# Nine instead of six feature tiles of an up projection by seven products, with sums and differences made sooner

## The chip, the cores and the metric

One NeuronCore of a Trainium2 chip runs the whole kernel in one launch. The metric is the device time of one execution in microseconds; the time before is the median of three runs.

## The reference

A hybrid encoder block on x of 512 positions by 1024 features in float32: three token mixers, merged and projected, then a gated feed-forward network with a convolution over the positions, then a norm. The change lies in the feed-forward part and the output projection ahead of it:

```python
x = x + merged @ w_out[l]
x = x + conv_glu_ffn(rms_norm(x, ffn_norm_g[l]), w_ffn_up[l], w_ffn_conv[l], b_ffn_conv[l], w_ffn_down[l])
return rms_norm(x, final_norm_g)

def conv_glu_ffn(h, w_up, w_conv, b_conv, w_down):
    a, u = jnp.split(h @ w_up, 2, axis=-1)        # 1024 -> 2 x 2816
    return (jax.nn.gelu(dwconv3(a, w_conv, b_conv)) * u) @ w_down
```

## The kernel before

**Arithmetic.** Every float32 product is made by three fp32r matmuls: each operand is split into a high part (a copy rounded by ACT) and a low part (the difference, by DVE), and `mm3` (L370 to L372) adds high x high, high x low and low x high. A weight block comes by an SP load into a raw buffer `wr` (three of them), is split into a `w` buffer (four of them) by ACT (L336) and DVE (L337), and is read by PE.

**Up projection.** The 2816 features of the gate half a (`ua`) and of the other half u (`uu`) are cut into 22 feature tiles f of 128. An ordinary tile takes 24 matmuls of 128x512 for `ua` and 24 for `uu`. Then comes the tail of the tile: the convolution (`conv`, L570 to L574), gelu on ACT (L1451), a multiplication with the norm's factor `rb2` on POOL, the product with u on DVE (L1467 or L1469), and from f = 12 on a split into UH and UL (L376, L377). Since a is done before u, most of the tail runs beside the `uu` matmuls.

A tile in `SUP` goes another way (`up_seven`): a and u are together a matrix product of 2 x 2 blocks (two halves of the features summed over, two halves of the positions, a and u), which seven products of half size replace, 7 x 12 = 84 matmuls of 128x256. Four of its weight operands are sums of blocks: `up_load` brings the first summand by SP into a tile `ut`, `up_sum` adds the second by an accumulating DMA on POOL's queue, and a fifth is a difference made on DVE. The differences of x are made once, by `x_forms(p)` for p = 0 to 3 (two ACT copies; DVE L1341, L1342, L1343; an ACT copy; DVE L1346, L1347), into units `xf`. In a tile of this kind a and u are complete only at its end.

**Down projection.** 62 blocks of `w_ffn_down` in the order `DOWN`: a "k" block multiplies one tile of UH/UL, an "s" block is part of a seven-product scheme over the first 12 tiles, some with an accumulated weight. Loads go out up to nine blocks ahead, into `wr` and then into quarters of *units* (14 buffers of 2112 floats a partition, `unit()`), which are also the home of x, its splits, its differences and the results. The first four blocks have six matmuls each. The residual is turned on the chip and kept in DRAM (`turn_out`, 64 KB stores) and brought back by eight 256 KB loads (`turn_in`, "U<-td" in the profile) for the sum at the end.

**What sets the order.** Each engine and each DMA queue issues in the order printed below; a scheduler places instructions by their place in the program and by what they wait for. `in_turn` keeps one engine's operations in program order. SP issues nearly all loads: a load that waits for its buffer holds back what stands behind it.

Of the kernel before, what the change touches and what calls it, by code (L numbers as in the profile page):

```python
# [25 lines left out]
NSP = 6  # L26
NOK = FT - 2 * NSP
HELD = 4
SUP = (5, 7, 9, 11, 13, 15)
UP_ORDER = (1, 2, 4, 5, 7, 3, 6)  # L30
HC = D // 2
NU = 14
# [105 lines left out]
def hybrid_block(ctx, tc, xT, memT, wflat, vecs, gbias, nabias, out):  # L138
# [21 lines left out]
    def scr(n=512):  # L160
        return sp.tile([P, 512], F32, tag="scr", name=nm("s"))[:, :n]
# [36 lines left out]
    def rstd_row_turned(u, tag):  # L198

        v, col, row = tiny(NT), tiny(32), tiny(32)  # L200
        G.memset(col, 0.0)
        V.tensor_reduce(v, u, axis=AX.XY, op=ALU.add)
        V.tensor_scalar(v, v, 1.0 / D, EPS, op0=ALU.mult, op1=ALU.add)
        G.tensor_tensor(col[:, :NT], v, nhalf[:, :NT], op=ALU.pow)
# [5 lines left out]
        SY.dma_start(rb, d.partition_broadcast(P))  # L210
        return rb

    def by4(a):
# [46 lines left out]
        q = slice(j * HC, (j + 1) * HC)  # L260
        return lw[0][:, q], lw[1][:, q]

    ur, uf = [], {}

    chain = {}

    def in_turn(eng, what, *a, **k):

        with tc.issue_after(chain[eng]) if eng in chain else ExitStack():
            chain[eng] = getattr({"V": V, "A": A, "G": G}[eng], what)(*a, **k).ins  # L270

    def emit_sum(i):

# [1038 lines left out]
    for f in range(KT):  # L1312
        xr = scr()
        SY.dma_start(xr, xT[:, f, :])
        ps = proj(("out", f), GH, GL)
        V.tensor_tensor(x2[f], ps, xr, op=ALU.add)
        split_act(HH[f], HL[f], x2[f], vcol("ffn_g", f))
        if f == 0:
            A.activation(acc2, x2[f], AF.Square)
        else:  # L1320
            sq = scr()
            A.activation(sq, x2[f], AF.Square)
            G.tensor_tensor(acc2, acc2, sq, op=ALU.add)


    x2v = [u[:, :4 * S].rearrange("p (f s) -> p f s", f=4) for u in x2u]
    ur.extend(unit() for _ in range(NSP // 2))
    ou, UH, UL = [], [], []
    res, turns = {}, {}
    xf = [unit(F32R) for _ in range(5)]  # L1330
    XF = (5, 2, 6, 7, 1)
    uw = {}

    def x_forms(p):

        y, d = ur[2][:, p % 2 * D:(p % 2 + 1) * D], ur[1][:, :5 * M]
# [4 lines left out]
        V.tensor_tensor(d5[:, 0:2], y4[:, 0:2], y4[:, 2:4], op=ALU.subtract)  # L1341
        V.tensor_tensor(d5[:, 2:4], y4[:, 1:3], y4[:, 0:4:3], op=ALU.subtract)  # L1342
        V.tensor_tensor(d5[:, 4], y4[:, 0], y4[:, 3], op=ALU.subtract)  # L1343
        h = xf[p][:, :5 * M]
        A.activation(h, d, AF.Copy)
        V.tensor_tensor(xf[p][:, 5 * M:8 * M], d[:, :3 * M], h[:, :3 * M].bitcast(F32), op=ALU.subtract)  # L1346
        V.tensor_tensor(xf[4][:, p * S:(p + 1) * S], d[:, 3 * M:], h[:, 3 * M:].bitcast(F32), op=ALU.subtract)  # L1347

    def x_of(i, p):

        if FORMS[i][1] is None:
            th, k = FORMS[i][0]
            q = slice(th * M, (th + 1) * M)
            return HH[2 * p + k][:, q], HL[2 * p + k][:, q]
        j = XF.index(i)
        lo = xf[p][:, (5 + j) * M:(6 + j) * M] if j < 3 else xf[4][:, p * S + (j - 3) * M:p * S + (j - 2) * M]
        return xf[p][:, j * M:(j + 1) * M], lo

    def up_load(f):

        for i in UP_ORDER:
            if ("ut", f, i) in BINDEX:
                off = BINDEX["ut", f, i][1]
                src = wflat[off:off + P * 2 * HC].rearrange("(p n) -> p n", p=P)
                r = tp.tile([P, S], F32, tag="E", name=nm("ut"), bufs=EB)
                SY.dma_start(r, src[:, :HC])
                uw[f, i] = r, src[:, HC:]

    def up_sum(f):
# [7 lines left out]
    def up_weight(f, n):  # L1377
# [13 lines left out]
        V.tensor_tensor(l, src, h.bitcast(F32), op=ALU.subtract)  # L1391
        uw[f, "w", i] = h, l

    def up_seven(f):

        b12, b45, b7, b36 = [atps() for _ in range(4)]
        at = {1: b12[:, :M], 2: b12[:, M:], 4: b45[:, :M], 5: b45[:, M:], 7: b7[:, :M], 3: b36[:, :M], 6: b36[:, M:]}
        ta, tu = scr(), scr()
        t00, t01, t11 = ta[:, :M], tu[:, :M], tu[:, M:]
        for n, i in enumerate(UP_ORDER):  # L1400
            if n + 2 < len(UP_ORDER):
                up_weight(f, n + 2)
            elif n + 2 == len(UP_ORDER):
                emit_split(st["split"])
                st["split"] += 1
            wh, wl = uw.pop((f, "w", i))
            for p in range(KT // 2):
                c = slice(p * P, (p + 1) * P)
                xh, xl = x_of(i, p)
                mm3(at[i], wh[:, c], wl[:, c], xh, xl, p == 0, p == KT // 2 - 1)  # L1410
            if i == 2:
                A.activation(ta, b12, AF.Copy)
                A.activation(t11, at[2], AF.Copy, scale=-1.0)
                V.tensor_tensor(t11, t11, at[1], op=ALU.add)
            elif i == 5:
                A.activation(t01, at[5], AF.Copy, scale=-1.0)
                t2 = ta.rearrange("p (u s) -> p u s", u=2)
                V.tensor_tensor(t2, t2, at[4].unsqueeze(1).to_broadcast([P, 2, M]), op=ALU.add)
                V.tensor_tensor(t00, t00, at[5], op=ALU.add)
            elif i == 7:  # L1420
                V.tensor_tensor(t00, t00, at[7], op=ALU.add)
            elif i == 6:
                V.tensor_tensor(tu, tu, b36, op=ALU.add)
                V.tensor_tensor(t11, t11, at[3], op=ALU.add)
        uw.pop(f)
        return ta, tu
    for f in range(FT):
        if f == 0:
            wa, wu = weights(("ua", f)), weights(("uu", f))
            pa, pu = mmps(), mmps()  # L1430
            for k in range(KT - 1):
                mm3(pa, wa[k][0], wa[k][1], HH[k], HL[k], k == 0, False)
            for k in range(KT - 1):
                mm3(pu, wu[k][0], wu[k][1], HH[k], HL[k], k == 0, False)
            t2 = turn_in(turn_out(by4(acc2)), "nab", 2)
            k = KT - 1
            mm3(pa, wa[k][0], wa[k][1], HH[k], HL[k], False, True)
            mm3(pu, wu[k][0], wu[k][1], HH[k], HL[k], False, True)
            pa1 = proj(("ua", 1), HH, HL, bank=atps)
            rb2 = rstd_row_turned(t2, "2")  # L1440
            pu1 = proj(("uu", 1), HH, HL, bank=atps)
        elif f in SUP:
            pa, pu = up_seven(f)
        else:
            if f + 1 in SUP:
                up_sum(f + 1)
            pa = pa1 if f == 1 else proj(("ua", f), HH, HL)
        if f + 2 in SUP:
            up_load(f + 2)
        c = conv(pa, rb2, "ffw", "ffb", f, FT)  # L1450
        A.activation(c, c, AF.Gelu_apprx_tanh)  # L1451
        if "G" not in chain:
            chain["G"] = G.tensor_tensor(c, c, rb2, op=ALU.mult).ins
        else:
            in_turn("G", "tensor_tensor", c, c, rb2, op=ALU.mult)
        if f < KT // 2:
            x_forms(f)
        if f > 0 and f not in SUP:
            if f + 1 in SUP:
                ws = weights(("uu", f))  # L1460
                uw[f + 1] = split.pop(BINDEX["ub", f + 1][0])
                for n in range(2):
                    up_weight(f + 1, n)
                split[BINDEX["uu", f][0]] = ws
            pu = pu1 if f == 1 else proj(("uu", f), HH, HL)
        if f < 2 * NSP:
            V.tensor_tensor(ur[f // 4][:, f % 4 * S:(f % 4 + 1) * S], pu, c, op=ALU.mult)  # L1467
        else:
            V.tensor_tensor(c, pu, c, op=ALU.mult)  # L1469
# [277 lines left out]
```

## Time and profile before

| | |
|---|---|
| median of three runs | 851.2 us (850.47 to 851.59) |
| profiled execution | 851.33 us, span 849.6 us, granted clock 0.999 |
| PE busy | 841.0 us (99% of the span) |
| DVE, ACT, POOL busy | 622.4, 476.4, 175.6 us |
| DMA | 147.32 MB, mean 173 GB/s |
| output projection | about 451.2 to 494.7 us |
| up projection | about 494.7 to 731.22 us |
| down projection | from 731.22 us |

How to read it: a row of a windows table is the window in us from the span's start, its length, then busy time and count of PE, PEld, DVE, ACT and POOL, the granted clock as a share, the share in which the DMA engines were busy, and GB/s. A row of a timeline is start, duration, engine, line, operation, output<-inputs; in brackets the engine's idle time ahead and what ended it. The rows of the chain of waits have start, duration, engine and operation. The rows of DMA issues have count, KB each and the median time from issue to landing.

### The profile page before, as it was taken

To read this page: it belongs to the slowest core of one execution; us is meant where nothing else is said; L and a number is where in the kernel's file an instruction comes from. 1 tells how busy PE (TensorE), PEld (TensorE's weight loads), DVE (VectorE), ACT (ScalarE), POOL (GpSimd) and SP (SyncE) were. 2 spreads that over 40 slices of the span, in tenths; PEclk is the share of its full clock that TensorE was granted. 3 is DMA by queue.
4 is the path that set the end of the run, shared out by engine and by line. 5 is a ranking of instruction groups with operands and counts; after the bars stand their busy time and mean duration, and the time that the engine had idled before them with its cause. 6 is when DMAs were issued, how large, how long until landed. Compare 5 with 4: busy or idle time off the path is not lost.

```text
span 849.6 us, 12743 instructions
## 1 busy us (share of the span) xinstructions
PE 841.0 (99%) x4214; PEld 716.3 (84%) x4214; DVE 622.4 (73%) x1246; ACT 476.4 (56%) x992; POOL 175.6 (21%) x268
## 2 busy tenths in 40 slices
PE   9999999999999999999999999999999999999997
PEld 8898988888888888888888888799999888888885
DVE  6699777766458748998676666877777856687893
ACT  7465557775446548888644644444455544444562
POOL 2000200000101840454000121423332111320421
PEclk9999999999999999999999999999999999999999
DMA  8236736563425856788743343588886333895882
GB/s 273 84 114 202 246 120 205 168 198 102 145 90 172 229 145 199 223 250 234 232 140 109 117 159 99 132 235 226 224 229 147 101 109 124 234 231 143 250 197 99
DMA packets 86226, 147.32 MB, mean 173 GB/s; under 512 B 11784, under 2 KB 38920, under 8 KB 86160
## 3 DMA queue, kind: packets, MB, share of 16 engines
q1 hardware_dynamic: 71600, 127.47, 46.9%
q0 software_dynamic: 14272, 18.90, 12.2%
q8 instruction: 33, 0.54, 0.3%
q14 instruction: 33, 0.27, 0.1%
q10 hardware_dynamic: 288, 0.14, 0.1%
HBM read 130.84 MB, written 15.62 MB: 172 GB/s over the span
## 4 chain that ended last, share of the span: by engine, by line
PE 91%; DMA 3%; DVE 2%; issue 2%; ACT 1%; POOL 0%; SPq 0%; POOLq 0%; DVEq 0%; ACTq 0%
PE mm L372 23%; PE mm L370 23%; PE mm L371 23%; PE at L372 6%; PE at L371 6%; PE at L370 6%; DMA s<-xT 2%; PE at L1033 1%; PE at L866 1%; PE at L868 1%; PE at L850 1%; DVE w L337 1%; PE at L404 0%; PE at L999 0%; PE at L1000 0%
## 5 line engine op out<-in xcount | busy, mean ns | idle before, releaser
L370 PE MATMUL mm<-u,w 128*128 128x512 f32 x763 | 298.8, 392 | 0.0
L372 PE MATMUL mm<-u,w 128*128 128x512 f32 x763 | 297.5, 390 | 1.0 <-DVE w L337 1.0
L371 PE MATMUL mm<-u,w 128*128 128x512 f32 x763 | 297.5, 390 | 0.0
L337 DVE TENSOR_TENSOR w<-wr,w 128x512 fp32r<-128x512 f32 (+2 forms) x233 | 159.8, 690 | 69.9 <-ACT w L336 68.5
L336 ACT ACTIVATE w<-wr 128x512 fp32r<-128x512 f32 (+2 forms) x232 | 144.8, 627 | 113.0 <-PE mm L372 72.2
L372 PEld LDWEIGHTS mm<-u,w 128*128 128x128 f32 x763 | 143.4, 188 | 32.0 <-DVE w L337 1.8
L371 PEld LDWEIGHTS mm<-u,w 128*128 128x128 f32 x763 | 143.5, 188 | 28.6
L370 PEld LDWEIGHTS mm<-u,w 128*128 128x128 f32 x763 | 143.5, 188 | 28.5
L679 POOL DMA_DIRECT2D u<-nav_d x128 | 62.3, 505 | 99.8 <-PE at L1033 52.3
L270 POOL TENSOR_TENSOR s<-s,rb 128x512 f32<-128x512 f32 x21 | 31.1, 1480 | 154.4 <-ACT s L1451 151.0
L372 PE MATMUL at<-u,w 128*128 128x256 f32 (+1 forms) x200 | 60.2, 301 | 0.0
L371 PE MATMUL at<-u,w 128*128 128x256 f32 (+1 forms) x200 | 60.0, 300 | 0.0
L370 PE MATMUL at<-u,w 128*128 128x256 f32 (+1 forms) x200 | 60.0, 300 | 0.0
L270 ACT ACTIVATE w<-u 128x512 fp32r<-128x512 f32 x52 | 32.7, 632 | 41.5 <-PE mm L372 20.6
L370 PE MATMUL mm<-w,u 128*128 128x512 f32 x128 | 50.4, 394 | 0.0
L372 PE MATMUL mm<-w,u 128*128 128x512 f32 x128 | 49.9, 390 | 0.0
L371 PE MATMUL mm<-w,u 128*128 128x512 f32 x128 | 49.9, 390 | 0.0
L270 DVE TENSOR_TENSOR w<-u,w 128x512 fp32r<-128x512 f32 x52 | 35.7, 688 | 18.1 <-ACT w L270 17.5
L572 ACT ACTIVATE s<-pad,vec 128x512 f32<-128x512 f32 x30 | 24.3, 812 | 27.6 <-DVE pad L570 24.3
L371 PEld LDWEIGHTS at<-u,w 128*128 128x128 f32 x200 | 38.2, 191 | 1.5
L370 PEld LDWEIGHTS at<-u,w 128*128 128x128 f32 x200 | 38.2, 191 | 1.5
L372 PEld LDWEIGHTS at<-u,w 128*128 128x128 f32 x200 | 38.2, 191 | 1.3
(333 smaller groups left out, 1390.3 us busy)
## 6 DMA issues: line engine op xcount, KB each, us to landing
wr<-wflat SPq DMA_DIRECT2D x118, 512.0 KB, 3.7
u<-wflat SPq DMA_DIRECT2D x50, 256.0 KB, 5.7
td<-s SPq DMA_DIRECT2D x172, 64.0 KB, 1.9
U<-td SPq DMA_DIRECT2D x41, 256.0 KB, 4.0
s<-xT SPq DMA_DIRECT2D x24, 256.0 KB, 4.0
ut<-wflat SPq DMA_DIRECT2D x24, 256.0 KB, 4.3
ut<-wflat POOLq DMA_DIRECT2D x24, 256.0 KB, 7.3
u<-wflat POOLq DMA_DIRECT2D x24, 256.0 KB, 7.6
```

The lines of the kernel that those rows point to most:

```text
L270: chain[eng] = getattr({"V": V, "A": A, "G": G}[eng], what)(*a, **k).ins
L336: A.activation(h[:, u:v], src, AF.Copy)
L337: V.tensor_tensor(l[:, u:v], src, h[:, u:v].bitcast(F32), op=ALU.subtract)
L370: PE.matmul(ps, lh, rh, start=start, stop=False)
L371: PE.matmul(ps, lh, rl, start=False, stop=False)
L372: st["mm"] = PE.matmul(ps, ll, rh, start=False, stop=stop).ins
L572: A.activation(t1, pad[:, 0:512], AF.Identity, scale=vcol(w, i), bias=vcol(b, i))
L679: G.dma_start(vw[r * 32:(r + 1) * 32, i * 256:(i + 1) * 256], nav_v[hf, r, CW[b]:CW[b] + 32, hp * 256:(hp + 1) * 256])
L850: PE.matmul(pv[:, i, 0:129], kt[:, d, i], va[:, i + d, h, 0:129], start=True, stop=True)
L866: PE.matmul(pv[:, d, 0:129], E[J // 2][:, 2 * (J % 2) + d, :], va[:, J, h, 0:129], start=True, stop=not inter)
L868: PE.matmul(pv[:, d, 0:129], Q[d][:, i, :], C[:, d, i, 0:129], start=False, stop=True)
L1033: PE.matmul(py[:, bl * 256:(bl + 1) * 256], vw[:, c:c + P], pp[bl][:, hf * 256:(hf + 1) * 256], start=hf == 0, stop=hf == 1)
```

## The change

Three further tiles, 17, 19 and 21, are made by seven products. Around that:

- The loads of the summands go out three tiles ahead (`up_load(f + 3)`), the accumulations two tiles ahead (`up_sum(f + 2)`); one summand of five goes to another buffer ("nab"). SP's loads of this kind keep the program's order.
- `x_forms(0)` is issued in the output projection behind its fourth tile, the others in tile 0.
- UH and UL of tiles 12 to 15 go where the residual's returned pieces were kept, and the residual comes back during the last two tiles, straight into two units.
- Two of the four PSUM banks of a seven-product tile come from the other pool.

```diff
-SUP = (5, 7, 9, 11, 13, 15)
+SUP = (5, 7, 9, 11, 13, 15, 17, 19, 21)
...
 for f in range(KT):
     xr = scr()
-        SY.dma_start(xr, xT[:, f, :])
+        chain["S"] = SY.dma_start(xr, xT[:, f, :]).ins
...
+        if f == 3:
+            x_forms(0)
...
-                r = tp.tile([P, S], F32, tag="E", name=nm("ut"), bufs=EB)
-                SY.dma_start(r, src[:, :HC])
+                tag, n = ("nab", 2) if i == 6 else ("E", EB)
+                r = tp.tile([P, S], F32, tag=tag, name=nm("ut"), bufs=n)
+                in_turn("S", "dma_start", r, src[:, :HC])
...
-        b12, b45, b7, b36 = [atps() for _ in range(4)]
+        b12, b45, b7, b36 = atps(), atps(), mmps(), mmps()
...
             t2 = turn_in(turn_out(by4(acc2)), "nab", 2)
+            x_forms(1)
...
             pa1 = proj(("ua", 1), HH, HL, bank=atps)
+            x_forms(2)
             rb2 = rstd_row_turned(t2, "2")
+            x_forms(3)
             pu1 = proj(("uu", 1), HH, HL, bank=atps)
...
-            if f + 1 in SUP:
-                up_sum(f + 1)
...
-        if f + 2 in SUP:
-            up_load(f + 2)
+            if f + 2 in SUP:
+                up_sum(f + 2)
...
+        if f + 3 in SUP:
+            up_load(f + 3)
...
-        if f < KT // 2:
-            x_forms(f)
...
-            if f % 2 == 0:
-                ou.append(unit(F32R))
-            for i, part in enumerate((UH, UL)):
-                a = f % 2 * 2 + i
-                part.append(ou[-1][:, a * S:(a + 1) * S])
+            if f < 2 * NSP + 4:
+                for tag, part in zip("HR", (UH, UL)):
+                    part.append(tp.tile([P, S], F32R, tag=tag, name=nm("UH"), bufs=4))
+            else:
...
-        if 6 <= f < 14:
-            t, g = (f - 6) % NT, (f - 6) // NT
-            res[t, g] = turn_in(turns[t, g], "HR"[g], 4)
+        if f >= FT - 2:
+            g, u = FT - 1 - f, unit()
+            for t in range(NT):
+                q = u[:, t * S:(t + 1) * S]
+                SY.dma_start(q, turns[t, g])
+                res[t, g] = q.rearrange("p (i s a) -> p s i a", i=4, a=32)
```

SP's queue at the end of the up projection, before: `wr_1240` is the last weight block of tile 21, `wr_1246` and the six behind it are blocks of the down projection, `u_1247` and `u_1275` units that take further blocks by quarters.

```order
L246 DMA wr_1231_7315<-wflat 128x1024
L246 DMA u_1247_7435<-wflat 128x512
L246 DMA wr_1236_7355<-wflat 128x1024
L246 DMA u_1247_7435<-wflat 128x512 x3
L246 DMA wr_1240_7391<-wflat 128x1024
L246 DMA wr_1246_7433<-wflat 128x512
L246 DMA wr_1254_7476<-wflat 128x512
L246 DMA u_1275_7583<-wflat 128x512
L246 DMA wr_1261_7522<-wflat 128x512
```

The same place in the changed kernel: `wr_1263` is tile 21's block, `wr_1264`, `wr_1273`, `wr_1300` and `wr_1301` are the first four blocks of the down projection, `wr_1307` is the fifth; `td` is the residual in DRAM, `gf` the final gain.

```order
L246 DMA wr_1263_7531<-wflat 128x1024
...
L246 DMA wr_1301_7771<-wflat 128x512
L246 DMA u_1265_7535<-wflat 128x512 x2
L1497 DMA u_1281_7626<-td_1072_6171 128x512
...
L1497 DMA u_1295_7758<-td_1056_6032 128x512
L1505 DMA gf_1299_7767<-gbias 128x512
L246 DMA u_1265_7535<-wflat 128x512 x2
L246 DMA wr_1307_7791<-wflat 128x512
L246 DMA u_1308_7793<-wflat 128x512
```

Between the fourth and the fifth block of the down projection now stand eight loads of the residual and the final gain; `u_1265` is the unit of `xf` that product 7 reads last.

DVE around tiles 2 and 3, before: `w_991` is the second half of tile 3's `ua` weights.

```order
L573 SCALAR_TENSOR_TENSOR s_988_5565<-pad0_150,vec_79,s_988_5565 128x512
L1346 TENSOR_TENSOR u_955_5339<-u_952_5336,u_955_5339 128x768
L1347 TENSOR_TENSOR u_958_5342<-u_952_5336,u_955_5339 128x512
L574 SCALAR_TENSOR_TENSOR s_988_5565<-pad0_150,vec_79,s_988_5565 128x512
L1341 TENSOR_TENSOR u_952_5336<-u_953_5337 128x512
L1342 TENSOR_TENSOR u_952_5336<-u_953_5337 128x512
L1343 TENSOR_TENSOR u_952_5336<-u_953_5337 128x256
L337 TENSOR_TENSOR w_991_5584<-wr_978_5466,w_991_5584 128x512
```

The same place in the changed kernel, where that half is `w_995`.

```order
L573 SCALAR_TENSOR_TENSOR s_992_5589<-pad0_150,vec_79,s_992_5589 128x512
L337 TENSOR_TENSOR w_995_5600<-wr_978_5498,w_995_5600 128x512
L574 SCALAR_TENSOR_TENSOR s_992_5589<-pad0_150,vec_79,s_992_5589 128x512
L337 TENSOR_TENSOR w_998_5635<-wr_984_5547,w_998_5635 128x512
L1477 TENSOR_TENSOR u_955_5347<-mm_996_5603,s_992_5589 128x512
```

The sets of differences now stand earlier, among the splits of the output projection and of tiles 0 and 1.

DVE at the end of tile 21 in the changed kernel: `s_1294` is its tail, `u_1280` its UH and UL, `w_1309` and `w_1312` are the splits of the fourth and fifth block of the down projection.

```order
L1437 TENSOR_TENSOR s_1287_7636<-s_1287_7636,mm_1285_7634 128x256
L573 SCALAR_TENSOR_TENSOR s_1294_7749<-pad1_153,vec_79,s_1294_7749 128x512
L270 TENSOR_TENSOR w_1309_7796<-wr_1301_7771,w_1309_7796 128x512
L574 SCALAR_TENSOR_TENSOR s_1294_7749<-pad1_153,vec_79,s_1294_7749 128x512
L270 TENSOR_TENSOR s_1310_7799<-u_905_5010 128x512
L1479 TENSOR_TENSOR s_1294_7749<-s_1287_7636,s_1294_7749 128x512
L377 SCALAR_TENSOR_TENSOR u_1280_7623<-s_1294_7749,u_1280_7623 128x512
L270 TENSOR_TENSOR w_1312_7811<-wr_1307_7791,w_1312_7811 128x512
```

In the kernel before, the fifth block's split stands behind tile 21's L377 as well, but there the tail's convolution starts when the gate half is done, 24 matmuls ahead of the tile's end; now it starts at the tile's end.

More of the change, by code (lines that the diff above doesn't have):

```diff
@@ L203, in rstd_row_turned @@
         V.tensor_scalar(v, v, 1.0 / D, EPS, op0=ALU.mult, op1=ALU.add)
-        G.tensor_tensor(col[:, :NT], v, nhalf[:, :NT], op=ALU.pow)
+        in_turn("G", "tensor_tensor", col[:, :NT], v, nhalf[:, :NT], op=ALU.pow)
         V.transpose(row, col)
@@ L209, in rstd_row_turned @@
         rb = cp.tile([P, S], F32, name=f"rb_{tag}", tag=f"rb{S}", bufs=2)
-        SY.dma_start(rb, d.partition_broadcast(P))
+        in_turn("S", "dma_start", rb, d.partition_broadcast(P))
         return rb
@@ L261, in lastw @@
         return lw[0][:, q], lw[1][:, q]
-    ur, uf = [], {}
+    uf = {}
     chain = {}
@@ L269, in in_turn @@
         with tc.issue_after(chain[eng]) if eng in chain else ExitStack():
-            chain[eng] = getattr({"V": V, "A": A, "G": G}[eng], what)(*a, **k).ins
+            chain[eng] = getattr({"V": V, "A": A, "G": G, "S": SY}[eng], what)(*a, **k).ins
     def emit_sum(i):
@@ L1311, in hybrid_block @@
     acc2 = cp.tile([P, S], F32, name="acc_2", tag="acc", bufs=1)
-    for f in range(KT):
-        xr = scr()
-        SY.dma_start(xr, xT[:, f, :])
[L1315 to L1330, printed above, removed]
     XF = (5, 2, 6, 7, 1)
-    uw = {}
+    uw, xf = {}, {}
+    ur = [None] + [unit() for _ in range(2)]
     def x_forms(p):
+        for q in (p, 4):
+            if q not in xf:
+                xf[q] = unit(F32R)
         y, d = ur[2][:, p % 2 * D:(p % 2 + 1) * D], ur[1][:, :5 * M]
@@ L1347, in x_forms @@
         V.tensor_tensor(xf[4][:, p * S:(p + 1) * S], d[:, 3 * M:], h[:, 3 * M:].bitcast(F32), op=ALU.subtract)
+    for f in range(KT):
+        xr = scr()
+        chain["S"] = SY.dma_start(xr, xT[:, f, :]).ins
+        ps = proj(("out", f), GH, GL)
+        V.tensor_tensor(x2[f], ps, xr, op=ALU.add)
+        split_act(HH[f], HL[f], x2[f], vcol("ffn_g", f))
+        if f == 0:
+            A.activation(acc2, x2[f], AF.Square)
+        else:
+            sq = scr()
+            A.activation(sq, x2[f], AF.Square)
+            chain["G"] = G.tensor_tensor(acc2, acc2, sq, op=ALU.add).ins
+        if f == 3:
+            x_forms(0)
+    x2v = [u[:, :4 * S].rearrange("p (f s) -> p f s", f=4) for u in x2u]
+    ur[0] = unit()
+    ur.extend(unit() for _ in range(NSP // 2 - 3))
+    ou, UH, UL = [], [], []
+    res, turns = {}, {}
     def x_of(i, p):
@@ L1392, in up_weight, with up_first @@
         uw[f, "w", i] = h, l
+    def up_first(f):
+        uw[f] = split.pop(BINDEX["ub", f][0])
+        for n in range(2):
+            up_weight(f, n)
     def up_seven(f):
-        b12, b45, b7, b36 = [atps() for _ in range(4)]
+        b12, b45, b7, b36 = atps(), atps(), mmps(), mmps()
         at = {1: b12[:, :M], 2: b12[:, M:], 4: b45[:, :M], 5: b45[:, M:], 7: b7[:, :M], 3: b36[:, :M], 6: b36[:, M:]}
@@ L1439, in hybrid_block @@
             pa1 = proj(("ua", 1), HH, HL, bank=atps)
+            x_forms(2)
             rb2 = rstd_row_turned(t2, "2")
+            x_forms(3)
             pu1 = proj(("uu", 1), HH, HL, bank=atps)
-        elif f in SUP:
-            pa, pu = up_seven(f)
-        else:
-            if f + 1 in SUP:
-                up_sum(f + 1)
-            pa = pa1 if f == 1 else proj(("ua", f), HH, HL)
-        if f + 2 in SUP:
-            up_load(f + 2)
+        else:
+            if f + 2 in SUP:
+                up_sum(f + 2)
+            if f in SUP:
+                pa, pu = up_seven(f)
+            else:
+                pa = pa1 if f == 1 else proj(("ua", f), HH, HL)
+        if f + 3 in SUP:
+            up_load(f + 3)
         c = conv(pa, rb2, "ffw", "ffb", f, FT)
         A.activation(c, c, AF.Gelu_apprx_tanh)
[L1452 to L1455, printed above, removed]
-        if f < KT // 2:
-            x_forms(f)
+        in_turn("G", "tensor_tensor", c, c, rb2, op=ALU.mult)
         if f > 0 and f not in SUP:
@@ L1460, in hybrid_block @@
                 ws = weights(("uu", f))
-                uw[f + 1] = split.pop(BINDEX["ub", f + 1][0])
-                for n in range(2):
-                    up_weight(f + 1, n)
+                up_first(f + 1)
                 split[BINDEX["uu", f][0]] = ws
@@ L1469, in hybrid_block @@
             V.tensor_tensor(c, pu, c, op=ALU.mult)
-            if f % 2 == 0:
-                ou.append(unit(F32R))
-            for i, part in enumerate((UH, UL)):
-                a = f % 2 * 2 + i
-                part.append(ou[-1][:, a * S:(a + 1) * S])
+            if f < 2 * NSP + 4:
+                for tag, part in zip("HR", (UH, UL)):
+                    part.append(tp.tile([P, S], F32R, tag=tag, name=nm("UH"), bufs=4))
+            else:
+                if f % 2 == 0:
+                    ou.append(unit(F32R))
+                for i, part in enumerate((UH, UL)):
+                    a = f % 2 * 2 + i
+                    part.append(ou[-1][:, a * S:(a + 1) * S])
             split_act(UH[-1], UL[-1], c)
```

## The prediction

> **What bounds the kernel now.** I read the page first: busy time, the chain that ended last, and the groups with their idle time.
>
> ```profile
> span 849.6 us, 12743 instructions
> PE 841.0 (99%) x4214; PEld 716.3 (84%) x4214; DVE 622.4 (73%) x1246; ACT 476.4 (56%) x992; POOL 175.6 (21%) x268
> PE 91%; DMA 3%; DVE 2%; issue 2%; ACT 1%; POOL 0%; SPq 0%; POOLq 0%; DVEq 0%; ACTq 0%
> L372 PE MATMUL mm<-u,w 128*128 128x512 f32 x763 | 297.5, 390 | 1.0 <-DVE w L337 1.0
> ```
>
> TensorE (PE) is busy 99% of the span and is 91% of the chain. So only two things move the time: PE work taken away, and holes in PE's stream that close or open. Next I cut the up projections and the stretch after them into windows, one tile or a known number of tiles each.
>
> ```profile
> 516.48:550.76 34.28, 33.23 (x145) 26.87 (x144) 28.73 (x46) 18.55 (x26) 11.48 (x9) 1.00 0.37 93
> 550.76:560.84 10.08, 10.08 (x86) 10.07 (x85) 7.54 (x14) 5.62 (x11) 1.48 (x1) 1.00 0.90 247
> 560.84:571.74 10.90, 10.90 (x50) 9.01 (x49) 8.88 (x15) 3.66 (x6) 5.14 (x5) 1.00 0.83 229
> 592.73:602.86 10.13, 10.13 (x86) 10.12 (x85) 7.62 (x14) 6.56 (x13) 1.31 (x1) 1.00 1.02 279
> 613.76:623.95 10.19, 10.19 (x86) 10.12 (x84) 7.62 (x14) 6.55 (x13) 1.31 (x1) 1.00 1.07 299
> 655.84:665.91 10.07, 10.07 (x86) 10.07 (x84) 8.47 (x15) 6.04 (x13) 1.55 (x1) 1.00 0.42 97
> 665.91:731.22 65.31, 65.31 (x291) 54.08 (x290) 42.64 (x63) 29.15 (x46) 8.75 (x7) 1.00 0.39 128
> ```
>
> The first number behind the window is its length, the second PE's busy time. 550.76:560.84 is tile 5 by seven products (84 matmuls 128x256), 560.84:571.74 is tile 6 by the ordinary way (48 matmuls 128x512), 592.73:602.86 and 613.76:623.95 are tiles 9 and 11, 655.84:665.91 is tile 15, and 665.91:731.22 holds tiles 16 to 21, all ordinary, without a hole. 516.48:550.76 is three ordinary tiles (2, 3, 4); it alone shows PE idle.
>
> **What the change gives.** Tiles 17, 19 and 21 go from ordinary to seven products. The last window is 65.31/6 = 10.885 us a tile, or 65.31/288 = 226.8 ns a matmul; tile 15 takes 10.07, or 119.9 ns for each of 84. Each converted tile saves 10.885 - 10.07 = 0.81 us; counting a pair as the trace has it (10.08 + 10.90 against 2 x 10.885) gives 0.79. Three tiles: -2.4 us. Tiles 9 and 11 run 0.05 and 0.11 over 10.08; with the sums of weights issued two tiles ahead instead of one I drop that: -0.15.
>
> The differences of x cost something at one place. The chain of waits and PE's own timeline there:
>
> ```profile
> 526.75 0.66 DVE s L573
> 527.41 0.86 DVE u L1346
> 528.28 0.60 DVE u L1347
> 529.47 0.68 DVE u L1341
> 530.15 0.60 DVE u L1342
> 530.75 0.33 DVE u L1343
> 531.08 0.61 DVE w L337
> 531.74 0.50 PE L372 MATMUL mm<-u,w 128*128 128x512 f32 x1 [1.05 <-DVE w L337]
> ```
>
> DVE works through a set of differences (L1346, L1347, then L1341 to L1343 of the next) before the low half of tile 3's weights (L337), and PE waits 1.05 us. The window 516.48:550.76 is 34.28 us for 144 matmuls, which at 226.8 ns are 32.66: 1.62 us of holes in all. In the changed order that split follows L573 directly, and the sets stand in the output projection and tiles 0 and 1. I take -1.4 back: the hole and most of the small ones. The ends: -1.62 if all go; and if the sets, 5 DVE operations of 0.4 to 0.9 us each, delay another split by as much in their new place, +0.2. What hides them there is DVE's idle time; if that is gone the same hole opens some 15 us sooner. The second statistic of the norm now queues behind the sets on SP and POOL by about 1 us; its first reader, tile 0's convolution, frees a PSUM bank that PE wants only tiles later, so nothing. The second queue past which something moves is POOL: with sums two tiles ahead each 256 KB accumulation has over 20 us to land. Nothing. Sum of the gains: -2.4 - 0.15 - 1.4 = -4.0 us.
>
> **What the change costs: the door to the down projection.** Call E the end of tile 21's products, where the down projection's first block begins. Before, tile 21 is ordinary and E comes at 731.22 with no hole behind it. Now two things end later than they did.
>
> First, tile 21's own tail. By seven products the gate half is complete only at E, so convolution, gelu, the multiplication with the norm, and the split all come behind E. Tile 15 shows that tail; its products end at 665.91 (DVE, ACT and POOL timelines):
>
> ```profile
> 666.16 0.68 DVE L1423 TENSOR_TENSOR s<-s,at 128x512 f32<-128x512 f32 x1
> 667.75 0.74 DVE L574 SCALAR_TENSOR_TENSOR s<-pad,vec,s 128x512 f32<-128x512 f32 x1
> 668.53 0.63 ACT L1451 ACTIVATE s<-s 128x512 f32<-128x512 f32 x1 [1.51 <-DVE s L574]
> 669.24 1.29 POOL L270 TENSOR_TENSOR s<-s,rb 128x512 f32<-128x512 f32 x1 [11.64 <-ACT s L1451]
> 671.00 0.68 DVE L1469 TENSOR_TENSOR s<-s,s 128x512 f32<-128x512 f32 x1
> 671.72 0.63 ACT L376 ACTIVATE u<-s 128x512 fp32r<-128x512 f32 x1 [2.03 <-DVE s L1469]
> 672.38 0.69 DVE L377 SCALAR_TENSOR_TENSOR u<-s,u 128x512 fp32r<-128x512 f32 x1
> 672.99 0.68 DVE L337 TENSOR_TENSOR w<-wr,w 128x512 fp32r<-128x512 f32 x1
> ```
>
> The tail is over at 672.99 + about 0.08, E + 7.1. In the changed order the split of the down projection's fifth block (tile w_1312 from the load wr_1307) stands behind L377 on DVE, and two more splits stand inside the tail (0.6 us each), so that split ends between E + 7.8 and E + 8.9. PE has four blocks of six matmuls before it, 24 x 0.2268 = 5.44 us, and one matmul of the fifth that needs no low half: it is due at E + 5.67. That alone is a hole of 2.1 to 3.2 us.
>
> Second, the load wr_1307. SP issues in order, and ahead of it stand: two quarters of a unit that product 7 of tile 21 still reads (free at about E - 2.85, 24 matmuls of 119.9 ns before E), eight 256 KB loads of the residual turned back (moved here from tiles 6 to 13), one 256 KB broadcast of the final gain, and two more quarters. It is the 14th transfer of 256 KB from E - 2.85.
>
> ```profile
> 8.00:14.00 6.00, 6.00 (x29) 4.94 (x28) 4.93 (x11) 4.69 (x8) 0.00 (x0) 1.00 1.04 378
> 734.00:748.00 14.00, 14.00 (x64) 11.59 (x63) 9.65 (x17) 6.98 (x13) 2.78 (x4) 1.00 1.09 261
> wr<-wflat SPq DMA_DIRECT2D x118, 512.0 KB, 3.7
> u<-wflat POOLq DMA_DIRECT2D x24, 256.0 KB, 7.6
> gf<-gbias SPq DMA_DIRECT2D x2, 256.0 KB, 3.9
> ```
>
> The last column of a window is GB/s. SP's loads alone, all 16 engines full, moved 378 (0.69 us for 256 KB); with POOL's accumulations beside them 261 (1.00). Such a load has a fixed part of 3.7 - 2 x 0.69 = 2.3 us. POOL's next accumulations wait for the 12th and 13th of the same loads, so I take 378: wr_1307 lands at E - 2.85 + 2.3 + 14 x 0.69 = E + 9.1. ACT's and DVE's halves of the split and the hand-offs, 0.63 + 0.68 + 0.2, make E + 10.6, against E + 5.67 due: a hole of 4.9 us. The ends: 2.1 if the load is early and only the tail counts; at 261 GB/s 4.4 more, 9.3.
>
> By the Trainium skill, "DMA: Bandwidth & Descriptors", section "Where 436 GB/s comes from", loads from HBM are held by about 358 GB/s a core; the 378 above says that this is not a hard ceiling here. By the page's figure the hole would be 0.6 us longer, an estimate, and the sum 852.8.
>
> Behind it: the ninth block of the down projection needs an accumulation on a quarter that lands 12th, at E + 7.7. With 7.6 us for the accumulation it is there at E + 15.4, and is due (60 matmuls, 4.9 us of hole, less 1.5 for the split) at E + 17.0; the one after it has 0 to 1 us to spare. I take +0.3; its ends are 0 and 2.5. The cover is the first hole itself: if that is short, this one grows, and the two together still come near 5. After it the down projection runs as before, where PE has no hole:
>
> ```profile
> 731.22:760.00 28.78, 28.78 (x128) 23.84 (x127) 21.71 (x35) 14.69 (x24) 9.07 (x11) 1.00 0.99 242
> 760.00:800.00 40.00, 40.00 (x177) 32.96 (x176) 32.55 (x55) 19.47 (x33) 6.52 (x6) 1.00 0.63 183
> ```
>
> So nothing behind the door takes up a late start there.
>
> **The sum.** -4.0 + 4.9 + 0.3 = +1.2. The profiled execution took 851.33 us and the median of the runs shown is 851.2; against the median: **852.4 us**, 0.14% more. What a measurement of this kernel can tell from no change is about 0.2%, 1.7 us: from 849.5 to 852.9 is "the same".
>
> **Rivals.**
> (1) The queue is not what holds the door: the loads that product 3 and product 7 release come sooner or faster, and only tile 21's tail counts, 2.1 to 3.2 us. Then 849.3 to 850.4. For it: the fixed part is a median of loads that did not queue. Against: none of the 14 transfers can start before E - 2.85, and 3.7 MB in the 7 us until they are needed would be over 500 GB/s, more than any window shows. It counts as faster only where the tail takes less than 2.4 us of hole.
> The Trainium skill says in "DMA: Bandwidth & Descriptors", section "Queues, rings and completion order", that completion is not first in, first out, so that a later load may finish before an earlier one; the rows here don't show the order of single pieces, and it would lean to this rival.
> (2) The other side, clearly slower: the accumulations meet the residual's loads. Price: at 261 GB/s wr_1307 lands 4.4 us later, 856.5; it decides as soon as the 14 loads take over 0.75 us each (+0.8 us). For it: 734:748 has just this mixture in just this place of the program. Against: POOL's accumulations wait for loads late in the same queue and for the tail's multiplication.
> (3) The hole at tile 3 does not go, only moves to the output projection or tile 1, where DVE has the sets to do instead: +1.4, 853.8.
> (4) Neither tail nor queue is seen by PE, because the order on the chip leaves slack I don't see: 851.2 - 4.0 = 847.2.
>
> **Chances.** The forecast's case (hole of 4 to 6 us) 0.42, of which 0.3 ends under 852.9; rival 1 0.22, split evenly about 849.5; rival 2 0.24; rival 3 0.08; rival 4 0.04. Faster 0.11 + 0.04 = 0.15; same 0.30 + 0.11 = 0.41, with 0.02 of the smaller cases of rival 3 0.43; slower the other 0.42. The forecast's own range is 851.4 to 853.5; for 8 in 10 it reaches to rival 1's middle, 849.8, and most of rival 2, 856.2.
>
> **What would show it.** Right: tiles 17, 19, 21 at about 10.07 us each with 119.9 ns a matmul; no wait at tile 3; the first stretch behind tile 21's last product with 24 matmuls, then a PE hole of 4 to 6 us whose releaser is the split of the fifth block (DVE or ACT) and behind it the DMA wr<-wflat with a landing over 6 us; residual loads landing between E and E + 8. Wrong: a hole under 3.5 us whose releaser is L377's successor alone (rival 1); loads of 10 us and more and a second hole about the ninth block (rival 2); a wait for DVE before tile 2 (rival 3); no hole (rival 4). What would upset the sum most is the rate at which those 14 transfers run: 0.1 us each is 1.4 us.

## The result and the profile after

The changed kernel takes 856.46 us (856.14 to 856.88), the kernel before 851.02: a ratio of 1.0062, interval 1.0047 to 1.0077. It is 5.4 us slower. The profiled execution spans 854.9 us against 849.6.

The windows of the changed kernel that answer to those of before: tiles 2 to 4; tiles 17 and 19; tile 21; the four blocks of the down projection behind it; the hole; nine matmuls; the stretch after them.

```profile
516.62:549.26 32.64, 32.64 (x146) 27.03 (x145) 21.66 (x34) 14.91 (x23) 9.55 (x9) 1.00 0.72 201
675.13:685.21 10.08, 10.08 (x86) 10.07 (x84) 8.45 (x15) 5.99 (x13) 5.13 (x5) 1.00 0.74 151
696.12:706.19 10.07, 10.07 (x86) 10.07 (x84) 8.43 (x15) 5.98 (x13) 5.18 (x5) 1.00 0.68 124
717.10:728.37 11.27, 10.37 (x85) 10.17 (x84) 8.55 (x16) 6.98 (x13) 1.31 (x1) 1.00 0.22 69
728.37:733.85 5.48, 5.48 (x26) 4.33 (x24) 4.88 (x9) 1.98 (x3) 0.46 (x1) 1.00 0.85 287
733.85:740.06 6.21, 0.15 (x1) 0.00 (x0) 1.40 (x3) 1.31 (x3) 2.27 (x3) 0.79 0.96 361
740.06:744.31 4.25, 4.25 (x9) 3.11 (x10) 3.77 (x6) 2.66 (x5) 3.09 (x5) 0.51 1.08 356
744.31:800.00 55.69, 55.69 (x247) 45.93 (x246) 42.41 (x68) 25.64 (x42) 7.83 (x9) 1.00 0.91 257
```

E is 728.37, 2.85 us earlier than the 731.22 of before. Behind it PE works 5.48 us, stands 6.21 us, and then runs nine matmuls at a granted clock of 0.51 in 4.25 us, where nine at 226.8 ns are 2.04. So: -2.85 + 6.21 + 2.21 = +5.57, against +5.3 of the spans. After 744.31 there is no hole.

The chain of waits over the hole (start, duration, piece), and ACT's timeline there:

```profile
728.46 5.10 DMA u<-td
...
733.62 5.68 DMA wr<-wflat
...
739.38 0.64 ACT w L270
...
740.06 0.80 PE mm L370
```

```profile
735.42 0.63 ACT L376 ACTIVATE u<-s 128x512 fp32r<-128x512 f32 x1 [2.11 <-DVE s L1479]
739.38 0.63 ACT L270 ACTIVATE w<-wr 128x512 fp32r<-128x512 f32 x1 [3.33 <-DMA wr<-wflat]
```

SP's queue up to that load (start, time of all issues of the row, count):

```profile
725.57 0.80 SPq L246 DMA_DIRECT2D u<-wflat  x2
726.42 4.52 SPq L1497 DMA_DIRECT2D u<-td  x8
731.50 0.33 SPq L1505 DMA_DIRECT2D gf<-gbias  x1
732.12 0.96 SPq L246 DMA_DIRECT2D u<-wflat  x2
733.62 0.33 SPq L246 DMA_DIRECT2D wr<-wflat  x1
```

The fifth block's load is issued at 733.62, when a residual load has landed (SP's loads share eight landing semaphores in turn, so each of these waits for the one issued eight before it), and lands at 739.30, E + 10.9. ACT has been done with tile 21's tail since 736.05 and waits 3.33 us for that load. So the load ends the hole, not the tail.

### The profile page after: what moved, and what is told of

Same layout as the page of the kernel before. It is cut to its first block, busy times and chain, and to the rows that moved or that the text cites. A ratio compares the mean times of both kernels' runs of the same rounds, so it can differ in the third digit from the quotient of the medians.

```text
span 854.9 us, 13057 instructions
## 1 busy us (share of the span) xinstructions
PE 840.7 (98%) x4322; PEld 720.8 (84%) x4322; DVE 637.8 (75%) x1276; ACT 483.9 (57%) x1010; POOL 186.7 (22%) x280
## 4 chain that ended last, share of the span: by engine, by line
PE 92%; DMA 3%; DVE 2%; ACT 1%; issue 1%; POOL 0%; SPq 0%; POOLq 0%; ACTq 0%; DVEq 0%
PE mm L370 23%; PE mm L371 23%; PE mm L372 23%; PE at L370 5%; PE at L372 5%; PE at L371 5%; DMA U<-td 1%; PE at L1033 1%; PE at L866 1%; DMA td<-s 1%; DMA wr<-wflat 1%; PE at L868 1%; PE at L850 1%; DMA u<-td 1%; PE at L404 0%
## 5 line engine op out<-in xcount | busy, mean ns | idle before, releaser
L370 PE MATMUL mm<-u,w 128*128 128x512 f32 (+1 forms) x823 | 310.9, 378 | 0.0
L371 PE MATMUL mm<-u,w 128*128 128x512 f32 (+1 forms) x823 | 309.4, 376 | 0.0
L372 PE MATMUL mm<-u,w 128*128 128x512 f32 (+1 forms) x823 | 309.4, 376 | 0.0
L337 DVE TENSOR_TENSOR w<-wr,w 128x512 fp32r<-128x512 f32 (+2 forms) x221 | 150.1, 684 | 58.8 <-ACT w L336 57.1
L336 ACT ACTIVATE w<-wr 128x512 fp32r<-128x512 f32 (+2 forms) x220 | 137.1, 626 | 84.4 <-PE mm L372 56.4
L372 PEld LDWEIGHTS mm<-u,w 128*128 128x128 f32 x823 | 155.0, 188 | 28.4
L371 PEld LDWEIGHTS mm<-u,w 128*128 128x128 f32 x823 | 155.3, 189 | 26.5
L370 PEld LDWEIGHTS mm<-u,w 128*128 128x128 f32 x823 | 155.3, 189 | 26.4
L372 PE MATMUL at<-u,w 128*128 128x256 f32 (+1 forms) x176 | 53.5, 304 | 0.9 <-DVE w L1398 0.9
L371 PE MATMUL at<-u,w 128*128 128x256 f32 (+1 forms) x176 | 53.3, 303 | 0.0
L370 PE MATMUL at<-u,w 128*128 128x256 f32 (+1 forms) x176 | 53.2, 302 | 0.0
L370 PE MATMUL mm<-w,u 128*128 128x512 f32 x96 | 37.9, 395 | 0.0
L372 PE MATMUL mm<-w,u 128*128 128x512 f32 x96 | 37.4, 390 | 0.0
L371 PE MATMUL mm<-w,u 128*128 128x512 f32 x96 | 37.4, 390 | 0.0
L372 PEld LDWEIGHTS at<-u,w 128*128 128x128 f32 x176 | 33.6, 191 | 2.4 <-DVE w L1398 1.1
L371 PEld LDWEIGHTS at<-u,w 128*128 128x128 f32 x176 | 33.6, 191 | 1.6
L370 PEld LDWEIGHTS at<-u,w 128*128 128x128 f32 x176 | 33.6, 191 | 1.6
```

The lines of the kernel that those rows point to most:

```text
L336: A.activation(h[:, u:v], src, AF.Copy)
L337: V.tensor_tensor(l[:, u:v], src, h[:, u:v].bitcast(F32), op=ALU.subtract)
L370: PE.matmul(ps, lh, rh, start=start, stop=False)
L371: PE.matmul(ps, lh, rl, start=False, stop=False)
L372: st["mm"] = PE.matmul(ps, ll, rh, start=False, stop=stop).ins
```

## The experiments

Each run stands beside runs of the kernel before on its own chip; ratios are to those (the median of before was 852.0, 851.3, 852.1 and 852.3 us in the four groups).

**The residual later.** The eight residual loads and the gain go out at the fourth block of the down projection.

```diff
-                SY.dma_start(q, turns[t, g])
+                back.append((q, turns[t, g]))
...
         wh, wl = weights(key)
+        if n == 3:
+            for a in back:
+                SY.dma_start(*a)
```

> The eight residual loads and the gain's second half go out at the fourth block of the down projection instead of ahead of the fifth block's load; nothing else is moved by hand. Theory Q (SP's queue makes the hole, the hole makes the slow clock): the fifth block's load is the 5th of 256 KB from E - 2.85, lands at about E + 3.4 (in the changed kernel E + 10.9), the hole of 6.2 us falls under 1 us and with it the 427 ns matmuls behind it (2.2 us): 856.5 - 8 = about 848.3 us. Rival T (tile 21's own tail is the floor): a hole of 2 to 3 us stays, 851 us, more if the clock still drops. Rival C (the slow matmuls come from the DMA traffic of that moment, not from the hole): the 2.2 us stay, 850.5.

854.71 us, 1.0029 (1.002 to 1.0039). The hole in front of the fifth block is gone, and no half clock is seen, but others come instead, some 5 us together between 738 and 758 (32.00 us hold 120 matmuls, which at 226.8 ns are 27.2), such as this one (PE's timeline, then POOL's, then the window with all of them):

```profile
745.45 0.39 PE L372 MATMUL at<-w,uf 128*128 128x512 f32 x1
746.85 0.49 PE L370 MATMUL at<-w,uf 128*128 128x512 f32 x1 [1.00 <-ACT w L270]
```

```profile
734.96 1.31 POOL L270 TENSOR_TENSOR s<-s,rb 128x512 f32<-128x512 f32 x1 [14.52 <-ACT s L1469]
736.21 3.57 POOL L270 DMA_DIRECT2D u<-wflat  x4
```

```profile
728.00:760.00 32.00, 29.00 (x120) 21.02 (x119) 20.61 (x34) 13.55 (x25) 6.69 (x8) 1.00 1.05 322
```

The queue's order made the first hole; with another order the accumulations, which POOL issues behind tile 21's multiplication, come too late. (With the load early the scheduler also put the fifth block's split ahead of the tail's last steps, so this run can't weigh the tail.)

**The accumulations sooner.** On top of that, POOL issues the two accumulations of the ninth and tenth block ahead of the multiplication.

```diff
+        if f == FT - 1:
+            while st["late"] <= DOWN0 + 9:
+                emit_raw(st["late"])
+                st["late"] += 1
+            while st["sum"] < st["late"]:
+                emit_sum(st["sum"])
+                st["sum"] += 1
         in_turn("G", "tensor_tensor", c, c, rb2, op=ALU.mult)
```

> The version with the residual's loads late, and POOL issues the accumulations of the ninth and tenth block ahead of tile 21's multiplication instead of behind it. Theory: what took back half of that version's gain (5 us of holes between E + 9 and E + 30) are accumulations that wait behind this multiplication, about 4 us; they go out at about E + 3.5, most of the holes between E + 14 and E + 20 close: 2 to 3.5 us faster than the version with the residual late (854.7), 851 to 852.5. Rival: the DMA engines are simply full there, the accumulations land no sooner, 854 to 855.

855.78 us, 1.0053 (1.0039 to 1.0068): a miss, and not on the rival's ground either. The accumulations went out at 731.90 and landed at 738.87 and 740.93, 4 to 5 us sooner. But then the residual was late, and DVE, whose order is fixed, stood in front of it with the splits behind:

```profile
746.67 1.33 DVE L270 TENSOR_TENSOR u<-u,at 128x512 f32<-128x512 f32 x2 [3.67 <-DMA u<-td]
```

```profile
748.65 0.79 PE L371 MATMUL at<-w,uf 128*128 128x512 f32 x1 [2.70 <-DVE w L270]
```

Three orders, three different latecomers. In the 25 us behind E the DMA engines moved 308, 313 and 322 GB/s in them, against 250 in the kernel before and 279 in the one with eight tiles further down, both without a hole there. That the stretch has more transfers than time is what the three suggest; it was not tested further.

**No residual loads.** POOL writes zeros in place of the eight loads; the residual is left out of the output.

```diff
-                SY.dma_start(q, turns[t, g])
+                G.memset(q, 0.0)
```

> The changed kernel with the eight residual loads replaced by zeros written by POOL: the residual is left out of the output, 2 MB fewer pass in the stretch behind E, tile 21 still by seven products. Theory D (the bytes that cannot start before tile 21 releases its units make the holes, in whatever order they go): no hole over 1 us before E + 30, ratio to before about 0.997 (gains of 2.9 us at E, 0.5 us of small holes). Rival T (tile 21's tail and the accumulations behind its multiplication): the accumulations still start at E + 7 and 2 to 4 us of holes stay, ratio 1.0 to 1.002.

853.31 us, 1.0016 (1.0007 to 1.0026). The 2 MB are worth about 4 us of the 5.4, but theory D in this strict form fell, and the ratio is the one that rival T had named (1.0 to 1.002). Holes remain: PE stands 4.4 us between 731 and 760, with DMA busy at 0.91. (This profiled execution took 856.14 us, 2.8 over the median, so its holes are larger than those of the median one.)

```profile
731.00:760.00 29.00, 24.64 (x100) 18.05 (x99) 19.13 (x31) 12.04 (x22) 7.84 (x9) 1.00 0.91 253
```

What is left are the loads and accumulations of the down projection itself. The fifth block's load had only five transfers ahead of it, was issued at 729.22 and still took 7.0 us to land. The accumulations went out at 738.78, E + 9.3, behind tile 21's multiplication, which on POOL's queue now waited for a load and came at E + 8.0 instead of E + 5.0. So this run does not part the bytes from the tail.

**The last tile ordinary.** Tiles 5 to 19, eight by seven products; all else as in the change.

```diff
-SUP = (5, 7, 9, 11, 13, 15, 17, 19, 21)
+SUP = (5, 7, 9, 11, 13, 15, 17, 19)
```

> The change with tiles 5 to 19 (eight tiles): tile 21 is ordinary, tile 3 too. Theory Q: no hole at the door (the differences of x are last read 11 us before E), none in the young phase, so the six-tile version's gain and two more tiles of 0.8: 0.9973 of before less 1.6 us, a ratio of about 0.9954 (848 us against 852). If the door's hole hangs on the number of seven-product tiles and not on tile 21 being one: 853 us and more.

848.06 us, 0.9956 (0.9941 to 0.9972): against the changed kernel's 1.0062, the conversion of tile 21 alone costs some 9 us. The same kernel once more, without an edit:

> The eight-tile version (5 to 19) once more, beside the nine-tile one on the same chip: ratio 0.9956 as before, within 0.001.

848.12 us, 0.9950 (0.9936 to 0.9964). This is the best version found; it beats both kernels. PE has no hole at the door. The reason shows in the last 16 us ahead of E (731.22 before, 728.37 changed, 728.06 with eight tiles):

```profile
715.22:731.22 16.00, 16.00 (x73) 13.24 (x72) 10.86 (x16) 7.56 (x12) 2.31 (x2) 1.00 0.47 146
```

```profile
712.37:728.37 16.00, 15.10 (x106) 14.08 (x105) 12.88 (x23) 9.12 (x17) 1.31 (x1) 1.00 0.21 65
```

```profile
712.06:728.06 16.00, 16.00 (x73) 13.24 (x71) 12.09 (x19) 8.26 (x13) 2.31 (x2) 1.00 0.68 216
```

With tile 21 by seven products the DMA engines move 65 GB/s there, 1.0 MB, because SP stands. Its waits in that stretch (engine and line, what released it, us):

```profile
SPq L246 <- DVE s L1427: 8.7, 1, 8.7
SPq L246 <- PE mm L372: 3.4, 1, 3.4
```

From 713.2 to 721.9 it stands before the raw buffer of the fourth block's load, which DVE's split of tile 21's own weights, the instruction ahead of L1427, is the last to read; then until 725.57 before the first unit of x's differences. The unit alone would have held it as long. With tile 21 ordinary the first unit is free at 703.47, 22 us sooner (tiles 20 and 21 lie between, not one tile as the expectation above has it), and 3.5 MB pass. The residual's return through the units costs nothing then.

**Six tiles.** The old list of tiles, all else as in the change.

```diff
-SUP = (5, 7, 9, 11, 13, 15, 17, 19, 21)
+SUP = (5, 7, 9, 11, 13, 15)
```

> The change with the old six tiles 5 to 15: sums two tiles ahead, differences of x sooner and the residual late remain, no tile is converted. Theory: the hole at tile 3 (1.5) and the 0.15 of tiles 9 and 11 go, the units are free long before E, so no hole at the door: 851.0 - 1.65 = 849.4 us. If the residual's late return costs by itself, whatever the units, 851 to 855.

849.64 us, 0.9973 (0.9961 to 0.9986), 2.3 us faster where 1.65 was expected, inside the interval. So the sooner differences and sums pay with no converted tile, and the residual's return during the last two tiles is free when the units are.

**Nine tiles in other places.** First 3, 5, ... 19, with the change as it is:

```diff
-SUP = (5, 7, 9, 11, 13, 15, 17, 19, 21)
+SUP = (3, 5, 7, 9, 11, 13, 15, 17, 19)
```

> Nine tiles by seven products again, but 3, 5, ... 19 instead of 5, 7, ... 21: tile 21 is ordinary, and the differences of x are last read 11 us before E, so the units are free sooner. The residual's loads stand where the change put them. Theory Q: the transfers are over before the fifth block is due, no hole, full clock; the same gains of 1.6 and 2.4 us: about 851.0 - 4.0 = 847 us. If the tile count itself had a price (more accumulating DMAs, the sums of tile 3 in a young phase) it shows as holes in tiles 2 to 20, 848 to 850 us.

853.02 us, 1.0011 (1.0 to 1.0021). No hole at the door, but one in tile 3, whose accumulations go out at 525.6 us behind a tile's multiplication on POOL:

```profile
531.14 0.58 PE L372 MATMUL at<-u,w 128*128 128x256 f32 x1 [2.76 <-DVE w L1398]
```

Then the same with tile 3's summands loaded in the output projection:

```diff
+    up_load(3)
     for f in range(FT):
...
+            up_sum(3)
             x_forms(3)
```

> Tiles 3, 5, ... 19 by seven products, with tile 3's summands loaded in the output projection and accumulated ahead of tile 0's multiplication (in the earlier version with these tiles the accumulations went out at 525.6 us and held PE 2.9 us, with the half clock behind it). Theory: this hole was the whole price of the ninth tile; without it the version is 0.8 us under the eight-tile one, ratio 0.9945 (847.4 against 852). Rival: the output projection's own loads are delayed by the four summands, or tile 3's split still comes late, a hole of 1 to 3 us stays, ratio 0.996 to 1.0.

854.20 us, 1.0027 (1.0015 to 1.0038), no faster than without. The accumulations now run beside the load of the norm's factor `rb2`, which takes 7.5 us instead of 3.3, all tails start late, and PE waits for a split behind them:

```profile
530.24 0.39 PE L370 MATMUL at<-u,w 128*128 128x256 f32 x1 [2.73 <-ACT w L1397]
```

Then 4, 6, ... 20:

```diff
-SUP = (5, 7, 9, 11, 13, 15, 17, 19, 21)
+SUP = (4, 6, 8, 10, 12, 14, 16, 18, 20)
```

> Nine tiles again, 4, 6, ... 20: the first is 11 us later than in the version with tile 3, whose accumulations came 3 us late, and the last is again ahead of an ordinary tile 21. Theory Q: neither hole, the whole gain of the change: eight-tile version less 0.8, ratio about 0.9945 (847.3 against 852). If the accumulations of the first tile are still late, a hole of up to 3 us with the half clock behind it: ratio 0.998 to 1.0.

850.86 us, 0.9988 (0.9979 to 0.9997): a hole of 2.0 us in front of the fifth block, whose load stands behind the residual again. And these tiles with the residual late, by the edit of the first experiment:

> Nine tiles 4, 6, ... 20 with the residual's loads behind the fifth block's load. In the version with the same tiles the fifth block's load stood behind 15 others and came 2 us late (half clock behind it). Theory: the load is early, the units are free since the end of tile 20, the rest has 10 us more than with tile 21: no hole, ratio 0.9950 (0.8 us under the eight-tile version). Rival D (the bytes are too many in this stretch): holes of 2 to 4 us come back between E + 9 and E + 25 as with tile 21, ratio 0.998 to 1.0.

852.48 us, 1.0005 (0.9997 to 1.0014). Its door is free, and a hole of 2.4 us with the half clock behind it comes at 743.7: the rival held, a little above its range. No order tried here gets the ninth tile for nothing.

**The clock.** 24 matmuls 128x512 without use, in the hole:

```diff
+        if n == 4:
+            for r in range(24):
+                st["mm"] = PE.matmul(px[r % NT], UH[0][:, :P], UH[1], start=True, stop=True).ins
```

> 24 matmuls 128x512 whose results are overwritten stand in the hole, between the fourth and the fifth block of the down projection; they write the banks that the fifth block starts afresh. They do no work. Theory Q: the wait for the load stays, but PE is busy through it, the clock stays full and the 2.2 us of 427 ns matmuls go: 854.3 us. Rival C (traffic slows the matmuls): the first nine real matmuls still take 427 ns, 856.5 us. If the fillers overrun the hole (24 x 0.227 = 5.4 us against 6.2) up to 0.5 us is lost again.

854.78 us, 1.0029 (1.0017 to 1.0041), some 2.8 us under the changed kernel by the ratios, and the real matmuls behind the hole start 0.23 us apart, not 0.43:

```profile
740.97 0.40 PE L371 MATMUL mm<-w,UH 128*128 128x512 f32 x1
741.21 0.39 PE L372 MATMUL mm<-w,UH 128*128 128x512 f32 x1
```

The DMA engines move as much as without the fillers (311 GB/s in the 25 us behind E, against 308). So idleness halves the clock, not the traffic. With 16 in place of 24:

```diff
-            for r in range(24):
+            for r in range(16):
```

> The filled hole with 16 idle-work matmuls instead of 24: 3.6 us of the hole are filled, a hole of about 2.6 us stays ahead of the fifth block. If the half clock follows only holes of 3 us and more, 854.8 us as with 24; if a hole of 2.6 us is enough, up to 2 us more, 855 to 857.

855.47 us, 1.0042 (1.0029 to 1.0056), its interval overlapping that with 24, so the times do not tell the two apart. The profile does, for its own execution: a hole of 2.52 us, and half the clock behind it.

```profile
737.60:740.12 2.52, 0.16 (x2) 0.00 (x1) 0.02 (x1) 0.68 (x2) 1.53 (x2) 0.95 1.05 403
740.12:743.27 3.15, 3.15 (x8) 2.48 (x8) 3.15 (x6) 2.66 (x5) 1.93 (x4) 0.50 1.07 384
```

## Why the prediction was wrong, step by step

Between the sum's +1.2 and the measured 5.4 us lie: the clock behind the hole, +2.2; a hole longer by 1.3; 1.2 inside tile 21; -0.2 at tile 3; and -0.3 for the late accumulation, which made no hole.

- **Seven products, -2.4.** Right for tiles 17 and 19 (10.08 and 10.07), and the 0.15 of tiles 9 and 11 came too (10.07 each). Tile 21 takes 11.27: 1.2 us that the prediction did not have, with PE waiting once:

```profile
721.33 0.38 PE L372 MATMUL at<-u,w 128*128 128x256 f32 x1 [0.90 <-DVE w L1398]
```

  The chain of waits shows its split behind the tail of tile 20 on DVE; the down projection's first splits stand there as well. It is in all six profiles with tile 21 converted and in none of the seven without; what makes it was not tested by itself.
- **The hole at tile 3, -1.4.** Right, and a little too careful: 34.28 us became 32.64. In the profiles of three experiments with the same order 0.2 to 1.0 us of it came back, so it is not gone for good.
- **"So nothing" for the norm's factor.** Right in this kernel, by luck rather than by reason: in the run with tile 3's sums sooner, where four accumulations went beside that load, it took 7.5 us and stood on the path.
- **The door, +4.9.** The right wait in the right place, under-sized: the load was put at E + 9.1 and landed at E + 10.9, and the hole was 6.2 us. (It would be longer still, but PE went on behind ACT's half of the split alone, 0.76 us after the landing, where the prediction had 1.5.) The start at E - 2.85 held (the first quarter goes out at 725.57). The mean was off: by the transfers' own times 725.57 to 739.30, less the 2.3 fixed, it is (13.73 - 2.3)/14 = 0.82 us a transfer for the 0.69 taken from a stretch where the engines are always full. But it was not the rate. What the engines moved from 725.5 to 740, in 40 slices:

```profile
GB/s 0 0 28 62 164 401 401 328 102 40 124 209 333 373 390 384 379 367 305 300 294 328 373 418 379 350 356 271 186 260 283 407 384 424 390 424 390 424 384 424
```

  The first two loads land at 728.47 and 729.21, where the sum had 728.5 and 729.2. Then there is a gap (40 to 124 GB/s from 728.4 to 729.5, with five loads issued): the third, issued at 726.42, lands at 731.42, 1.5 us late, and the eleven behind it follow at 0.72 us each. The run without residual loads has a longer gap (its third load lands 3.7 us behind the second), so the residual does not make it; what does is not shown. The figure of 358 GB/s in the Trainium skill, "DMA: Bandwidth & Descriptors", section "Where 436 GB/s comes from", would have brought the term 0.6 us nearer, an estimate (with it the prediction's sum is 853.0, not 852.8). Over the whole time, gap included, these loads ran at 320 here (256 KB in 0.82 us).
- **The tail as a floor, 2.1 to 3.2.** Not the bound in this kernel (ACT's 3.33 us of waiting for the load). What it would cost alone stays open: the scheduler moved the split in each version whose load was early.
- **What follows the hole.** The step that failed most: the sum ended with the hole and put what follows it at nothing, without a reason. PE's clock at half behind it adds 2.2 us. It was foreseeable: the Trainium skill, "TensorE: Matmul & The Clock Gate", section "Part 1: The HAM clock gate (the "warmup" mystery)", says that the clock halves after an idle window of about 3.4 us and comes back after one of work. The trace agrees: 6.21 us of idleness, then 426 to 427 ns a matmul for 4 us.
- **Why the forecast's case was wrong at all.** Rival 2 had named 856.5 us, but for accumulations that meet the residual's loads; they went out at 738.60, too late to have done it. Its sign, over 0.75 us for each of the 14 loads, came true on the mean (0.82), but that made the load 1.8 us late, not 4.4. The price was right by accident. What the rivals lacked is the common cause: tile 21 by seven products holds a raw buffer until 721.9 and the units of x's differences to its end, so that the loads, the residual and the accumulations of the next 25 us all start at one moment. That tile 21 is the cause the eight-tile runs show; that it acts through these buffers is read from SP's waits and was not tested by itself. The prediction priced one of the transfers at a time.

## What to carry to other kernels

A change that saves PE time in the last tile of a phase also moves the moment when its buffers come free; ask what the next phase could load before that moment, and count all of it against the DMA engines, not only the transfer that waits first. Compare the bytes moved ahead of the boundary with those that the stretch behind it needs. In the 16 us ahead of E the versions without a hole behind it moved 214 to 216 GB/s, the two with tile 20 last, with holes of 2.0 and 2.4 us, 155, those with tile 21 by seven products 65 to 68. The kernel before moved only 146 and had no hole, but it needed less behind E: its residual had come back long before. And price a hole of PE with the clock behind it: 6 us cost 8.

## What was not expected of the hardware

Holes shorter than the 3.4 us of the Trainium skill ("TensorE: Matmul & The Clock Gate", the section named above) brought the half clock too: 2.5 us here with 16 fillers, and 2.0 us in the nine even tiles. There PE was back at work for 0.57 us at full clock before the half clock came, and it stayed 3.41 us:

```profile
732.84:734.87 2.03, 0.16 (x1) 0.00 (x1) 0.02 (x1) 0.68 (x2) 0.87 (x1) 1.00 1.05 396
734.87:735.44 0.57, 0.57 (x2) 0.48 (x3) 0.57 (x1) 0.47 (x1) 0.16 (x1) 1.00 1.15 273
735.44:738.85 3.41, 3.41 (x10) 2.67 (x9) 3.08 (x6) 2.19 (x4) 1.01 (x2) 0.50 1.08 320
738.85:742.00 3.15, 3.15 (x15) 2.63 (x14) 0.95 (x3) 1.44 (x3) 1.88 (x3) 1.00 1.10 259
```

A hole of the same 2.0 us (734.99 to 736.99) in the run without residual loads brought none (0.51 us for the next matmul, then full speed), nor did those of 1.0 to 1.4 us. The same section of the Trainium skill says that the window runs free of what PE does. The traces agree: the half clock starts on marks of a fixed step, not at the end of a hole. In the nine even tiles it starts at 735.44 and again, after PE's last work, at 848.08, which is 33 steps of 3.413 us; in the changed kernel at 737.40 and 853.46, 34 steps of 3.413. So a hole of about 2 us falls either way by where it lies between two marks. The eleven executions of the nine even tiles fit that: four had a mean granted clock of 0.999 or more and took 849.25 to 850.39 us, seven had 0.996 to 0.998 and took 850.54 to 851.31. How much idleness between two marks it takes, no run here fixes.
